# Add and GELU on 1024 x 4096: stores moved to ScalarE's queue, and every transfer in rows of 4 KB

## The chip, the cores and the metric

The kernel runs on one core of a Trainium2 chip. The metric is the device time of a run in microseconds. Each profile is of one execution; its span goes from the first to the last instruction, and the device time of that execution is a little longer than the span.

## The reference

```python
def reference(x, y):            # both float32, 1024 x 4096
    z = x + y
    return 0.5 * z * (1 + np.tanh(np.sqrt(2 / np.pi) * (z + 0.044715 * z ** 3)))
```

It is one elementwise chain: two tensors of 16.78 MB are read and one of 16.78 MB is written. The tanh form is computed as z * sigmoid(2 * sqrt(2/pi) * (z + 0.044715 z^3)), which is the same function.

## The kernel before

The 1024 rows are spread over 128 partitions, 8 rows to each, so that a partition owns 32768 elements that lie together in memory (128 KB). The elements of a partition are cut twice.

For the transfers they are cut into tiles by the list `sizes` (L43): 1024, 1024, 2048, then six tiles of 4096, then 2048, 1024, 512, 512 elements per partition, 13 tiles in all. A tile of 4096 elements is 2 MB, and one of its transfers has 128 rows of 16 KB. `load_x` (L71) loads a tile of x into a buffer of its own, which nothing else uses. `load_y` (L75) loads into one of four buffers of 4096 elements; a buffer is used again once its adds are done. `store` (L82) writes the x tile, which by then holds the result.

For the computation they are cut into chunks of at most 1024 elements. Each chunk passes five steps: `add` (L92), z = x + y, on Pool (GpSimd) for all but the first two and last two chunks, which VectorE adds; `sq` (L97), a scaled square on ScalarE into one of four PSUM buffers; `stt` (L100), (square + c1) * z on VectorE; `sig` (L105), the sigmoid on ScalarE; and `mul` (L108), sigmoid * z on VectorE, which puts the result into the x tile.

The order on every engine is written out by hand in four lists (L111 to L131) and kept as written. SyncE's list `sp` holds all transfers: x and y loads of tile after tile, and between them the stores. `LEAD` (8192 elements) says when: a store is put behind the loads that reach at least that far beyond it. VectorE's and ScalarE's lists come from one loop over i: VectorE gets `stt(i)`, `mul(i-1)` and, for the few chunks that Pool leaves, `add(i+3)`; ScalarE gets `sig(i)` and `sq(i+2)`. An instruction whose input is not there holds up everything behind it on its engine.

Of the kernel before, what the change touches and what calls it, by code (L numbers as in the profile page):

```python
# [1 line left out]

# [1 line left out]

# [4 lines left out]


@with_exitstack
def kernel(
    ctx: ExitStack,
    tc: tile.TileContext,
    x: bass.AP,
    y: bass.AP,
    out: bass.AP,
):

    nc = tc.nc
    P = nc.NUM_PARTITIONS
    fp32 = mybir.dt.float32
    act = mybir.ActivationFunctionType
    alu = mybir.AluOpType  # L30

    N, D = x.shape
    assert N % P == 0
    NB = N // P
    TOT = NB * D

    c1 = 2.0 * math.sqrt(2.0 / math.pi)
    root = math.sqrt(c1 * 0.044715)

    LEAD = 8192  # L40
    CH = 1024
    YB = 4
    sizes = [1024, 1024, 2048] + [D] * (NB - 2) + [2048, 1024, 512, 512]  # L43
    assert sum(sizes) == TOT
    starts = [sum(sizes[:t]) for t in range(len(sizes))]
    T = len(sizes)

    def hbm(ap, t):
        v = ap.rearrange("(p n) d -> p (n d)", p=P)
        return v[:, starts[t] : starts[t] + sizes[t]]  # L50

    chunks = []
    for t in range(T):
        o = 0
        while o < sizes[t]:
            f = min(CH, sizes[t] - o)
            chunks.append((t, o, f))
            o += f
    C = len(chunks)
    last = {t: c for c, (t, _, _) in enumerate(chunks)}  # L60
    by_pool = set(range(2, C - 2))

    xpool = ctx.enter_context(tc.tile_pool(name="xz", bufs=1))
    ypool = ctx.enter_context(tc.tile_pool(name="y", bufs=YB))
    ppool = ctx.enter_context(
        tc.tile_pool(name="w", bufs=4, space=bass.MemoryType.PSUM)
    )

    xt, yb, yt, wt = {}, {}, {}, {}

    def load_x(t):  # L71
        xt[t] = xpool.tile([P, sizes[t]], fp32, tag=f"x{t}", name=f"x{t}")
        nc.sync.dma_start(out=xt[t], in_=hbm(x, t))  # L73

    def load_y(t):  # L75
        n, o = divmod(starts[t], D)
        if o == 0:
            yb[n] = ypool.tile([P, D], fp32, tag="y", name=f"y{n}")
        yt[t] = yb[n][:, o : o + sizes[t]]
        nc.sync.dma_start(out=yt[t], in_=hbm(y, t))  # L80

    def store(t):  # L82
        nc.sync.dma_start(out=hbm(out, t), in_=xt[t])  # L83

    def z(c):
        t, o, f = chunks[c]
        return xt[t][:, o : o + f]

    def add(c):
        t, o, f = chunks[c]  # L90
        eng = nc.gpsimd if c in by_pool else nc.vector
        eng.tensor_add(out=z(c), in0=z(c), in1=yt[t][:, o : o + f])  # L92

    def sq(c):
        f = chunks[c][2]
        wt[c] = ppool.tile([P, CH], fp32, tag="w", name=f"w{c}")[:, :f]
        nc.scalar.activation(out=wt[c], in_=z(c), func=act.Square, scale=root)  # L97

    def stt(c):
        nc.vector.scalar_tensor_tensor(  # L100
            out=wt[c], in0=wt[c], scalar=c1, in1=z(c), op0=alu.add, op1=alu.mult
        )

    def sig(c):
        nc.scalar.activation(out=wt[c], in_=wt[c], func=act.Sigmoid)  # L105

    def mul(c):
        nc.vector.tensor_mul(out=z(c), in0=wt[c], in1=z(c))  # L108


    sp, pool, dve, acts = [], [], [], []  # L111
    s = 0
    for t in range(T):
        sp += [(load_x, t), (load_y, t)]
        while s < T and starts[s] + sizes[s] + LEAD <= starts[t] + sizes[t]:
            sp.append((store, s))
            s += 1
    sp += [(store, t) for t in range(s, T)]
    for c in range(C):
        if c in by_pool:  # L120
            pool.append((add, c))
    for i in range(-3, C + 1):
        if 0 <= i < C:
            dve.append((stt, i))
            acts.append((sig, i))
        if 0 <= i - 1 < C:
            dve.append((mul, i - 1))
        if 0 <= i + 3 < C and i + 3 not in by_pool:
            dve.append((add, i + 3))
        if 0 <= i + 2 < C:  # L130
            acts.append((sq, i + 2))  # L131

    needs = {
        load_x: lambda t: [],
        load_y: lambda t: [
            (add, c)
            for c, (i, _, _) in enumerate(chunks)
            if starts[t] % D == 0 and starts[i] // D == starts[t] // D - YB
        ],
        add: lambda c: [(load_y, chunks[c][0]), (load_x, chunks[c][0])],  # L140
        sq: lambda c: [(add, c)] + ([(mul, c - 4)] if c >= 4 else []),
        stt: lambda c: [(sq, c)],
        sig: lambda c: [(stt, c)],
        mul: lambda c: [(sig, c)],
        store: lambda t: [(mul, last[t])],
    }
    queues = [sp, pool, acts, dve]
    done = set()
    with tc.manual_schedule():
        one = xpool.tile([P, 1], fp32, tag="one", name="one")  # L150
        nc.vector.memset(one, 0.0)  # L151
        nc.scalar.activation(out=one, in_=one, func=act.Sigmoid)  # L152
        while any(queues):
            moved = False
            for q in queues:
                while q and all(n in done for n in needs[q[0][0]](q[0][1])):
                    fn, arg = q.pop(0)
                    fn(arg)
                    done.add((fn, arg))
                    moved = True  # L160
                    if q is not sp:
                        break
            assert moved, [q[:1] for q in queues]


# [1 line left out]
_INS = ['x', 'y']  # L167
_OUTS = [((1024, 4096), 'float32')]


# [23 lines left out]
```

## Time and profile before

| | |
|---|---|
| time, median of 2 runs | 126.73 us (126.62 to 126.85) |
| the profiled execution | 126.61 us |
| its span | 124.8 us |
| VectorE busy | 79.1 us, 71 instructions |
| Pool busy | 67.4 us, 33 instructions |
| ScalarE busy | 64.2 us, 68 instructions |
| DMA | 50.33 MB, 96.7% of 16 engines' span |
| one transfer of 2 MB, issue to landing (median) | x 18.5, y 23.3, store 14.0 us |

In the profile DVE is VectorE, ACT is ScalarE, POOL is GpSimd, and SP is SyncE; SPq is SyncE's queue of transfers. A number such as L92 is a line of the kernel. The rows of digits are 40 equal slices of the span, each digit the busy share in tenths, with the moved GB/s beneath. In a table by windows each row begins with the window in us and its length, then the busy time of VectorE, ScalarE and Pool with the instructions in it, then the TensorE clock, the DMA share and the GB/s. A row of a group shows how often it ran, its total busy time, the mean ns of one, and the idle time ahead of it with what ended it.

### The profile page before, as it was taken

To read this page: it belongs to the slowest core of one execution; us is meant where nothing else is said; L and a number is where in the kernel's file an instruction comes from. 1 tells how busy PE (TensorE), PEld (TensorE's weight loads), DVE (VectorE), ACT (ScalarE), POOL (GpSimd) and SP (SyncE) were. 2 spreads that over 40 slices of the span, in tenths; PEclk is the share of its full clock that TensorE was granted. 3 is DMA by queue.
4 is the path that set the end of the run, shared out by engine and by line. 5 is a ranking of instruction groups with operands and counts; after the bars stand their busy time and mean duration, and the time that the engine had idled before them with its cause. 6 is when DMAs were issued, how large, how long until landed. Compare 5 with 4: busy or idle time off the path is not lost.

```text
span 124.8 us, 301 instructions
## 1 busy us (share of the span) xinstructions
DVE 79.1 (63%) x71; ACT 64.2 (51%) x68; POOL 67.4 (54%) x33
## 2 busy tenths in 40 slices
DVE  0159259049979970299703996059930699899960
ACT  4036084068857820578206881088800887684610
POOL 0000670599799603996049950699207998960000
DMA  4999999999899999999999999999999999999494
GB/s 88 417 437 452 433 431 420 425 420 420 345 461 433 425 415 415 431 441 431 425 425 441 420 425 431 441 436 425 425 412 410 417 415 411 450 420 425 184 392 165
DMA packets 5618, 50.35 MB, mean 403 GB/s; under 512 B 624, under 2 KB 624, under 8 KB 2544
## 3 DMA queue, kind: packets, MB, share of 16 engines
q1 hardware_dynamic: 5616, 50.33, 96.7%
q14 instruction: 2, 0.02, 0.0%
HBM read 33.55 MB, written 16.78 MB: 403 GB/s over the span
## 4 chain that ended last, share of the span: by engine, by line
DMA 64%; POOL 15%; DVE 11%; SPq 3%; ACT 2%; issue 2%; POOLq 0%
DMA y<-in_y_dram 64%; POOL x L92 15%; DVE x L108 5%; DVE w L100 5%; SPq L73 2%; ACT w L97 2%; DVE x L92 1%; SPq L80 1%; ACT w L105 0%; SPq L83 0%; POOLq L92 0%
## 5 line engine op out<-in xcount | busy, mean ns | idle before, releaser
L92 POOL TENSOR_TENSOR x<-x,y 128x1024 f32<-128x1024 f32 x29 | 67.2, 2346 | 43.7 <-DMA y<-in_y_dram 43.7
L100 DVE SCALAR_TENSOR_TENSOR w<-w,x 128x1024 f32<-128x1024 f32 (+1 forms) x33 | 39.5, 1198 | 34.3 <-ACT w L97 34.3
L97 ACT ACTIVATE w<-x 128x1024 f32<-128x1024 f32 (+1 forms) x33 | 33.1, 1002 | 51.5 <-POOL x L92 45.1
L108 DVE TENSOR_TENSOR x<-w,x 128x1024 f32<-128x1024 f32 (+1 forms) x33 | 39.0, 1181 | 0.1
L105 ACT ACTIVATE w<-w 128x1024 f32<-128x1024 f32 (+1 forms) x33 | 31.6, 958 | 3.5 <-DVE w L100 3.4
L92 DVE TENSOR_TENSOR x<-x,y 128x1024 f32<-128x1024 f32 (+1 forms) x4 | 4.9, 1231 | 6.3 <-DMA y<-in_y_dram 6.3
L152 ACT ACT_TABLE_LOAD x1 | 1.3, 1283 | 0.7 <-PEq L178 0.7
L151 DVE MEMSET one<- 128x1 f32 x1 | 0.1, 59 | 0.8 <-PEq L178 0.8
L178 POOL MEMSET const-float32-0.0<- 128x1 f32 x1 | 0.1, 98 | 0.2 <-issue 0.2
L152 ACT ACTIVATE one<-one 128x1 f32<-128x1 f32 x1 | 0.2, 202 | 0.0
L178 POOL MEMSET const-bfloat16-1.0<- 128x1 bf16 x1 | 0.1, 101 | 0.0
L178 POOL MEMSET const-uint8-127<- 128x1 uint8 x1 | 0.1, 101 | 0.0
L178 POOL MEMSET const-float32-1.0<- 128x1 f32 x1 | 0.1, 98 | 0.0
## 6 DMA issues: line engine op xcount, KB each, us to landing
x<-in_x_dram SPq DMA_DIRECT2D x6, 2048.0 KB, 18.5
y<-in_y_dram SPq DMA_DIRECT2D x6, 2048.0 KB, 23.3
out_dram<-x SPq DMA_DIRECT2D x6, 2048.0 KB, 14.0
x<-in_x_dram SPq DMA_DIRECT2D x2, 1024.0 KB, 12.3
y<-in_y_dram SPq DMA_DIRECT2D x2, 1024.0 KB, 14.3
out_dram<-x SPq DMA_DIRECT2D x2, 1024.0 KB, 7.0
x<-in_x_dram SPq DMA_DIRECT2D x3, 512.0 KB, 5.4
y<-in_y_dram SPq DMA_DIRECT2D x3, 512.0 KB, 6.2
```

Of the source, the lines that this page charges most:

```text
L73: nc.sync.dma_start(out=xt[t], in_=hbm(x, t))
L80: nc.sync.dma_start(out=yt[t], in_=hbm(y, t))
L92: eng.tensor_add(out=z(c), in0=z(c), in1=yt[t][:, o : o + f])
L97: nc.scalar.activation(out=wt[c], in_=z(c), func=act.Square, scale=root)
L100: nc.vector.scalar_tensor_tensor(out=wt[c], in0=wt[c], scalar=c1, in1=z(c), op0=alu.add, op1=alu.mult)
L105: nc.scalar.activation(out=wt[c], in_=wt[c], func=act.Sigmoid)
L108: nc.vector.tensor_mul(out=z(c), in0=wt[c], in1=z(c))
L151: nc.vector.memset(one, 0.0)
L152: nc.scalar.activation(out=one, in_=one, func=act.Sigmoid)
L178: nc = _bacc.Bacc("TRN2", target_bir_lowering=False, num_devices=1)
```

## The change

`sizes` becomes 32 tiles of 1024 elements, so that each transfer is 512 KB in 128 rows of 4 KB, and a tile is a chunk. `store` is issued by ScalarE's queue in place of SyncE's. SyncE's list then holds loads alone, and `LEAD` is gone. ScalarE's list gets the stores: `store(i-3)` after `sq(i+2)`, and the last two at the end. The buffers of y still hold 4096 elements, four tiles each. The five steps of a chunk, their engines and their order stay as they are, with all chunks now 1024 elements long; before, the last two had 512.

```diff
-    LEAD = 8192
     CH = 1024
     YB = 4
-    sizes = [1024, 1024, 2048] + [D] * (NB - 2) + [2048, 1024, 512, 512]
+    sizes = [CH] * (TOT // CH)
...
     def store(t):
-        nc.sync.dma_start(out=hbm(out, t), in_=xt[t])
+        nc.scalar.dma_start(out=hbm(out, t), in_=xt[t])
...
     sp, pool, dve, acts = [], [], [], []
-    s = 0
     for t in range(T):
         sp += [(load_x, t), (load_y, t)]
-        while s < T and starts[s] + sizes[s] + LEAD <= starts[t] + sizes[t]:
-            sp.append((store, s))
-            s += 1
-    sp += [(store, t) for t in range(s, T)]
...
         if 0 <= i + 2 < C:
             acts.append((sq, i + 2))
+        if 0 <= i - 3 < C:
+            acts.append((store, i - 3))
+    acts += [(store, t) for t in range(C - 2, C)]
```

## The prediction

> **What bounds the kernel now.** I read the page's first parts, then busy time by windows, then the queue's waits and the groups. The page first: engine shares, and the DMA rows in 40 slices of 3.12 us.
>
> ```profile
> span 124.8 us, 301 instructions
> DVE 79.1 (63%) x71; ACT 64.2 (51%) x68; POOL 67.4 (54%) x33
> ...
> DMA  4999999999899999999999999999999999999494
> GB/s 88 417 437 452 433 431 420 425 420 420 345 461 433 425 415 415 431 441 431 425 425 441 420 425 431 441 436 425 425 412 410 417 415 411 450 420 425 184 392 165
> ...
> q1 hardware_dynamic: 5616, 50.33, 96.7%
> ```
>
> No compute engine passes 63%; the 16 DMA engines are full from the second slice to the thirty-seventh. Three tensors of 16.78 MB (50.33 MB) have to pass, so only the rate, the head and the tail can move the time. The windows, with the DMA share and GB/s in the last two columns, separate these:
>
> ```profile
> 4.00:6.50 2.50, 0.61 (x1) 0.00 (x0) 0.00 (x0) 1.00 1.03 421
> 30.00:36.00 6.00, 5.93 (x6) 4.15 (x5) 5.13 (x4) 1.00 1.00 385
> 36.00:38.00 2.00, 1.20 (x2) 1.68 (x2) 2.00 (x2) 1.00 1.13 475
> 48.00:60.00 12.00, 7.70 (x7) 7.67 (x8) 9.26 (x4) 1.00 1.01 433
> ...
> 100.00:103.00 3.00, 3.00 (x4) 2.63 (x4) 3.00 (x2) 1.00 0.99 406
> ...
> 116.00:118.00 2.00, 2.00 (x3) 1.79 (x3) 0.00 (x0) 1.00 0.28 119
> 118.00:122.00 4.00, 2.57 (x4) 0.76 (x2) 0.00 (x0) 1.00 0.98 396
> 122.00:124.80 2.80, 0.00 (x0) 0.00 (x0) 0.00 (x0) 1.00 0.37 139
> ```
>
> Clean stretches of 16 KB rows give 433 GB/s. The first loads, in 4 KB rows, give 421; 100 to 103 us, which mixes 4 and 8 KB rows, gives 406. Where the first stores follow loads the rate dips to 385 for 6 us and then catches up at 475. The last 8.8 us carry 119x2.0 + 396x4.0 + 139x2.8 = 2.21 MB. The 48.12 MB before that took 116.0 less a head of 2.5 us (the first slice's 88 GB/s x 3.12 us = 0.275 MB, at 421 worth 0.65 us, so data flows as if from 2.5): 113.5 us, a mean of 424.
>
> The transfer queue's waits:
>
> ```profile
> SPq L83 <- DVE x L108: 86.0, 12, 14.1
> SPq L73 <- DMA y<-in_y_dram: 5.4, 1, 5.4
> ```
>
> The queue spends most of its time standing at a store until `mul` has finished, which costs nothing while earlier transfers fill the engines. The second row matters more: a load of x into a buffer of its own needs no data, yet waited for a y load to land. [...] The groups give the durations used below:
>
> ```profile
> L92 POOL TENSOR_TENSOR x<-x,y 128x1024 f32<-128x1024 f32 x29 | 67.2, 2346 | 43.7 <-DMA y<-in_y_dram 43.7
> L100 DVE SCALAR_TENSOR_TENSOR w<-w,x 128x1024 f32<-128x1024 f32 x31 | 38.1, 1231 | 34.3 <-ACT w L97 34.3
> L108 DVE TENSOR_TENSOR x<-w,x 128x1024 f32<-128x1024 f32 x31 | 37.6, 1213 | 0.0
> L97 ACT ACTIVATE w<-x 128x1024 f32<-128x1024 f32 x31 | 31.9, 1028 | 51.5 <-POOL x L92 45.1 <-DVE x L92 6.4
> L105 ACT ACTIVATE w<-w 128x1024 f32<-128x1024 f32 x31 | 30.5, 983 | 2.1 <-DVE w L100 2.0
> ```
>
> [...] The trace has nothing of two queues (all data is in q1). [...]
>
> **The change, part by part.** *Rows of 4 KB.* All 96 transfers become 512 KB. In the trace one 4 KB row takes 159 ns on its engine, a 16 KB row 611, so four small ones cost 25 ns (4%) more. By the rows' durations alone the small ones give 16 x 4096 B / 159 ns = 412 GB/s; what was moved gives 406 to 421. I take 415, and keep 406 and 424 as bounds.
>
> *Semaphores and prefetch.* In the order of the changed program, loads run up to tile 7, then every third transfer is a store. [...]the x load of tile s+10 waits for the landing of store s, and the y load of tile t for the x load of tile t-2. Four or five loads of 512 KB can then be queued, over two tiles' time, so the engines stay fed as long as the store returns in time. A tile takes 3 x 0.524 MB / 415 = 3.79 us. Store s stands in ScalarE's queue behind `sq` of tile s+5, so it is issued 2.35 (Pool add) + 1.03 (`sq`) + about 0.4 = 3.8 us after tile s+5 lands. From then to the landing of tile s+9, the last load that is free to go, are 4 x 3.79 = 15.2 us. The store should take 2.7 fixed (a lone 512 KB store in the tail of before takes 4.0 to land, 1.26 of it data) and two data times, since it shares, 5.2 us; the freed load needs another 2.7. 3.8 + 5.2 + 2.7 = 11.7 < 15.2: covered by 3.5 us.
>
> *Issuing on ScalarE.* 32 issues at 0.33 to 0.69 us (the range on SyncE; ScalarE's isn't shown), I take 0.4. Queued behind each is `sig`, on which `mul` waits. Per tile 1.03 + 0.98 + 0.4 = 2.4 us of 3.8: hidden in the body at either bound; VectorE (2.44) and Pool (2.35) are under 3.8 too. Against before, SyncE no longer stands at a store, but as the queue was full that frees no time.
>
> *The tail.* This is where I see the loss. Let E be the landing of y31, the last load. ScalarE's order is fixed: sq30, store 25, sig29, sq31, store 26, sig30, store 27, sig31, stores 28 to 31. VectorE, not Pool, adds tiles 30 and 31, and has add31 ahead of stt29. So after E: add31 ends at 1.2, stt29 at 2.5, sig29 at 3.5, sq31 at 4.5, and only then does store 26 go, whose `mul` ended long ago. VectorE goes on: mul28 3.7, stt30 4.9, mul29 6.1, stt31 7.3; sig31 ends at 8.3; then stores 28 to 31 are issued. Store 25 goes near E+1, 26 near 4.5, 27 near 6: the engines are mostly idle until then. From 8.3: 2.7 fixed + 4 x 1.26 data + 0.8 to the end of the span (as before's last landing at 124.0 to 124.8) = E+16.85.
>
> *The sum.* By the last byte of the loads, 64 loads and 25 stores have passed: 89 x 0.524 = 46.66 MB. At 415 that is 112.4 us. With the head 2.5 and 1.0 from last byte to landing (an estimate, within the 2.7), E = 115.9; the span is 132.7. The profiled run of before took 126.61 for a span of 124.8, so 1.8 is added: 134.5 us. That run lies 0.1 below the median of 126.73, which I neglect. Against before: the body sheds 1.46 MB (-3.4 us), the rows cost 2.4 (415 for 424), and the tail is 17.85 instead of 8.8 (+9.05). At 424 the result is 132.1, at 406 it is 137.2.
>
> **The rivals.** *Alternating directions costs.* If switching from load to store packet by packet keeps the dip's 385 GB/s: 46.66/385 = 121.2, in all 143.7. For it: the dip. Against: 475 just after, so what a switch one way loses, the way back returns.
>
> *Loads starve behind the semaphores.* If a store takes 12 us to land because loads are ahead of it on every engine, five tiles need 3.8 + 12 + 2.7 + 1.3 = 19.8, so 3.95 us per tile, 0.16 more for some 26 tiles: 138.7. It decides from 8.7 us of landing time.
>
> *Directions overlap (the other side).* If loads and stores use separate paths and the body reaches the 475 of that one window: 98.2 us, and 17.3 of tail: 119.8, faster. It decides from 456 GB/s (124.2). [...]475 was a catch-up.
>
> *Nearly no change.* If 4 KB rows run at the 433 of long ones and the tail is 1.6 us shorter (landing at 0.3, and stores 25 to 27 spread better): 107.8 + 2.5 + 16.2 + 1.8 = 128.3.
>
> **How the numbers follow.** Likeliest case 0.54 (132 to 137), costly alternation 0.17, starved loads 0.12, no change 0.10, overlap 0.07. Two per cent is about what a measurement of this kernel can tell from no change, 124.2 to 129.3. So faster 0.07, same 0.10, slower 0.83. The range 129.0 to 143.5 leaves out the overlap, most of the no-change case and what of the alternation lies above it.
>
> **What would show it.** Right: two data queues, with a DMA share near 1.0 and 406 to 424 GB/s until about 114 us, then some 17 us in which the slices alternate low and full, and ScalarE waiting for VectorE's stt with stores behind. Compute groups keep their durations. Wrong: slices above 440 in the body (overlap), 4 KB packets far longer than 159 ns (alternation), or SyncE waiting for store landings with a share below 0.95 (starved). A tail that is full to the end would make my largest term wrong.

## The result and the profile after

The changed kernel takes 131.75 us (131.67 to 131.82, 2 runs) against 126.73: a ratio of 1.0395, 95% interval 1.0349 to 1.0442. It is slower by 4%. The forecast was 134.5 with a range of 129.0 to 143.5; the time lies in it, just under the 132 to 137 of the likeliest case. The profiled execution took 131.82 us for a span of 130.0.

The first parts of its page, in the same form as before:

```profile
span 130.0 us, 345 instructions
DVE 79.9 (61%) x69; ACT 64.0 (49%) x66; POOL 65.9 (51%) x32
...
DMA  4999999999999999999999999999999999954594
GB/s 102 417 418 408 410 413 407 403 421 418 422 417 418 422 421 418 421 416 423 418 418 421 416 423 420 416 420 417 420 423 417 420 416 422 420 218 161 214 404 188
...
q1 hardware_dynamic: 9216, 33.56, 64.0%
q10 hardware_dynamic: 4608, 16.78, 31.7%
```

The data now passes through two queues, loads in q1 and stores in q10. The busy times of the compute engines are what they were, ScalarE's included, though it now issues 32 transfers. The body is level between 403 and 423 GB/s, where before it moved between 345 and 461. The new thing stands at the end: slices 36, 37 and 38 at 218, 161 and 214 GB/s. The windows say how much that is (last two columns: DMA share and GB/s):

```profile
110.00:115.00 5.00, 3.29 (x3) 0.89 (x1) 0.00 (x0) 1.00 0.88 360
115.00:124.00 9.00, 8.84 (x9) 5.01 (x6) 0.00 (x0) 1.00 0.53 211
124.00:128.00 4.00, 0.55 (x1) 0.00 (x0) 0.00 (x0) 1.00 1.02 408
```

From 115 to 124 us VectorE is busy for 8.84 of 9 us and the DMA engines for half of the time. Measured against 419 GB/s, the first two rows lack 0.7 + 4.5 = 5.2 us of transfer time. The hole of the kernel before, 119 GB/s from 116 to 118 us, lacks 1.4 against its mean of 424. In these windows the tail lost 3.7 us more than it did. Counted from 110 us to the end of each span, where the means are 271 and 314 GB/s, it is 3.2. The timeline shows what those microseconds held (start, duration, engine, line, operation; ACTq is ScalarE's sequencer, which issues its transfers):

```profile
111.71 1.23 DVE L91 TENSOR_TENSOR x<-x,y 128x1024 f32<-128x1024 f32 x1 [6.28 <-DMA y<-in_y_dram]
...
115.36 1.23 DVE L91 TENSOR_TENSOR x<-x,y 128x1024 f32<-128x1024 f32 x1 [0.16 <-DMA y<-in_y_dram]
...
117.76 1.01 ACT L104 ACTIVATE w<-w 128x1024 f32<-128x1024 f32 x1 [1.71 <-DVE w L99]
117.77 0.34 ACTq L82 DMA_DIRECT2D out_dram<-x  x1
...
122.29 1.01 ACT L104 ACTIVATE w<-w 128x1024 f32<-128x1024 f32 x1 [1.25 <-DVE w L99]
122.29 2.91 ACTq L82 DMA_DIRECT2D out_dram<-x  x4
```

The first two rows are the adds of tiles 30 and 31; the second is released by the last load. The next two are the sigmoid of tile 29 and, with it, the store of tile 26. The last two are the sigmoid of tile 31 and the last four stores, 28 to 31: the first of them is issued at 122.29 us, the last at 124.6, when its product is done. Until 122.29 us the engines get one store at a time.

### The profile page after: what moved, and what is told of

Same layout as the page of the kernel before. It is cut to its first block, busy times and chain, and to the rows that moved or that the text cites. A ratio compares the mean times of both kernels' runs of the same rounds, so it can differ in the third digit from the quotient of the medians.

```text
span 130.0 us, 345 instructions
## 1 busy us (share of the span) xinstructions
DVE 79.9 (61%) x69; ACT 64.0 (49%) x66; POOL 65.9 (51%) x32
## 4 chain that ended last, share of the span: by engine, by line
DMA 81%; DVE 7%; POOL 4%; SPq 3%; issue 1%; POOLq 0%; DVEq 0%; ACT 0%
DMA y<-in_y_dram 41%; DMA x<-in_x_dram 30%; DMA out_dram<-x 10%; POOL x L91 4%; DVE x L107 3%; DVE w L99 3%; SPq L72 1%; SPq L79 1%; DVE x L91 1%; POOLq L91 0%; DVEq L91 0%; ACT w L96 0%
## 5 line engine op out<-in xcount | busy, mean ns | idle before, releaser
L91 POOL TENSOR_TENSOR x<-x,y 128x1024 f32<-128x1024 f32 x28 | 65.7, 2347 | 42.8 <-DMA y<-in_y_dram 42.6
L99 DVE SCALAR_TENSOR_TENSOR w<-w,x 128x1024 f32<-128x1024 f32 x32 | 39.4, 1232 | 30.7 <-ACT w L96 30.6
L96 ACT ACTIVATE w<-x 128x1024 f32<-128x1024 f32 x32 | 32.9, 1027 | 50.8 <-POOL x L91 44.1
L107 DVE TENSOR_TENSOR x<-w,x 128x1024 f32<-128x1024 f32 x32 | 38.9, 1216 | 0.0
L104 ACT ACTIVATE w<-w 128x1024 f32<-128x1024 f32 x32 | 31.5, 985 | 7.7 <-DVE w L99 7.4
L91 DVE TENSOR_TENSOR x<-x,y 128x1024 f32<-128x1024 f32 x4 | 4.9, 1225 | 13.1 <-DMA y<-in_y_dram 13.1
```

The lines of the kernel that those rows point to most:

```text
L99: nc.vector.scalar_tensor_tensor(out=wt[c], in0=wt[c], scalar=c1, in1=z(c), op0=alu.add, op1=alu.mult)
```

## The experiments

Two things were to be settled. Which part of the loss belongs to the rows, the second queue and the tail? And in the tail: are finished stores held up in ScalarE's queue, as the prediction argued, or is too little left to store when the last load lands? Ratios are to the kernel before, run beside each.

**Short rows alone.** The kernel before, with each of its transfers cut:

```diff
-        nc.sync.dma_start(out=xt[t], in_=hbm(x, t))
+        nc.sync.dma_start(out=xt[t], in_=hbm(x, t), max_dma_last_dim=4096)
```

and the same on the y loads and the stores.

> The kernel before with its 13 tiles, one queue and its order, but every transfer cut into rows of 4 KB (a 2 MB transfer has 512 rows in place of 128). It has the row length alone. Theory (rows cost a little everywhere): the clean stretches fall from 433 to about 418 GB/s as in the changed kernel, so 48 MB take 2 to 4 us longer: 128.7 to 130.7 us, a 4 KB row still 159 ns. Rival (the whole loss is in the tail and the flat 419 GB/s of the changed kernel comes from mixing loads with stores): the body keeps 433 GB/s and the time stays at 126.7.

128.05 us, ratio 1.0114 (1.0059 to 1.0168). The windows:

```profile
12.00:30.00 18.00, 8.50 (x9) 7.16 (x9) 10.52 (x5) 1.00 1.03 409
50.00:56.00 6.00, 2.41 (x3) 3.11 (x4) 5.84 (x3) 1.00 1.03 424
118.00:120.00 2.00, 2.00 (x4) 1.31 (x3) 0.00 (x0) 1.00 0.86 352
```

Short rows cost 1.1%, some 1.4 us, under the 2 to 4 that the theory gave, so its range is missed by a little; the rival's unchanged time and 433 GB/s are further off. The first window holds loads alone, the second stores: both below the 433 of long rows, the loads further. The third row bears on the small sum: the hole of the tail, 119 GB/s with long rows, is 352 here. That the slower body fills part of it is my reading, not tested by itself.

**The second queue alone.** The tiles and long rows of before, the stores on ScalarE three chunks behind `sq`; SyncE's list loses its stores, as in the changed kernel:

```diff
-        nc.sync.dma_start(out=hbm(out, t), in_=xt[t])
+        nc.scalar.dma_start(out=hbm(out, t), in_=xt[t])
...
+        acts += [(store, t) for t in range(T) if last[t] == i - 3]
+    acts += [(store, t) for t in range(T) if last[t] > C - 3]
```

> The tiles and long rows of the kernel before, with the stores issued by ScalarE three chunks behind sq, as in the changed kernel. It has the second queue and the mixing alone. Theory (mixing loads and stores is free, the tail costs): 425 to 433 GB/s until the last load lands at about 113 us, then a tail of 12 to 14 us with half-empty slices, 127 to 129 us. Rival (alternation costs): the body falls below 410 GB/s and the time goes to 131 us or more. Rival (mixing gains): the body is above 440 GB/s.

126.91 us, ratio 1.0053 (1.0032 to 1.0075), just under the 127 to 129 expected. From 48 to 60 us it moves 437 GB/s, and 427 over the 100 us from 4 to 104:

```profile
48.00:60.00 12.00, 9.28 (x8) 7.77 (x8) 7.07 (x4) 1.00 1.02 437
4.00:104.00 100.00, 65.62 (x57) 54.08 (x56) 63.06 (x28) 1.00 1.01 427
```

The kernel before has 433 and 425 in the same two windows. Loads and stores under way together thus neither cost nor gain anything to speak of; both rivals on this fall. The 0.5% by which the run is longer goes with a hole near its end, taken up below.

**Stores held back.** The changed kernel, its stores five tiles later, the backlog released together before the sigmoid of tile 29:

```diff
+        if i == C - 3:
+            acts += [(store, t) for t in range(C - 11, C - 4)]
...
-        if 0 <= i - 3 < C:
-            acts.append((store, i - 3))
-    acts += [(store, t) for t in range(C - 2, C)]
+        if 0 <= i - 8 < C - 11:
+            acts.append((store, i - 8))
+        if i >= C - 2:
+            acts.append((store, i - 2))
+    acts += [(store, t) for t in range(C - 1, C)]
```

> The changed kernel with its stores held back five tiles more (store of tile i-8 in place of i-3), and the seven held ones, 21 to 27, released together ahead of the sigmoid of tile 29; 28 to 31 follow as their products are done. Nothing else. Theory (in the changed kernel the loads end too late, with too few stores left to cover the last tiles' arithmetic): the last load lands about 109 us, the engines stay full over the tail, 50.33 MB at 417 GB/s, 126 to 127 us. Rival (4 KB rows and mixing are the whole loss): the time stays at 130 us or above.

128.02 us, ratio 1.0121 (1.0054 to 1.0188). That is 3.7 us less than the changed kernel by the medians, 3.5 by the ratios, and 1 above the expectation.

```profile
span 126.1 us, 346 instructions
...
DMA  3999999999999999999999999999999999899994
GB/s 83 418 422 407 413 411 407 409 412 409 407 414 417 418 422 421 416 420 418 422 418 420 420 420 418 416 421 417 421 417 418 422 420 417 339 403 404 408 403 182
...
105.61 1.22 DVE L91 TENSOR_TENSOR x<-x,y 128x1024 f32<-128x1024 f32 x1 [5.59 <-DMA y<-in_y_dram]
```

The half-empty slices are gone; what is left is one at 339. The add of tile 30, which waits for its y load in every variant, starts at 105.61 us in place of 111.71. Five stores of 0.524 MB at 419 GB/s are 6.3 us: holding five stores back let the loads end 6 us sooner, and the held stores covered the arithmetic. The time is now that of short rows alone (1.0114).

**Stores moved up.** The changed kernel, with the opposite edit:

```diff
+        if 0 <= i - 2 < C:
+            acts.append((store, i - 2))
         if 0 <= i < C:
             acts.append((sig, i))
...
-        if 0 <= i - 3 < C:
-            acts.append((store, i - 3))
-    acts += [(store, t) for t in range(C - 2, C)]
+    acts += [(store, t) for t in range(C - 1, C)]
```

> The changed kernel with each store moved up ScalarE's list, ahead of the sigmoid two tiles later (store i-2 before sig i), so that no store stands behind a sigmoid that waits for VectorE. Nothing else. Theory as the prediction had it (finished stores held up behind sig29, sq31, sig30 make the idle slices): 2 us or more are saved, below 129.8 us. Rival (the tail is set by the last load and by VectorE's seven steps after it; earlier stores only delay the last load by their own bytes): between 131 and 133 us.

132.59 us, ratio 1.0476 (1.0419 to 1.0532). It is not faster, as it would be if held-up stores were the cause. That it is slower than the changed kernel is only indicated, since the intervals overlap by a little. The timeline and the windows:

```profile
114.25 1.23 DVE L91 TENSOR_TENSOR x<-x,y 128x1024 f32<-128x1024 f32 x1 [6.23 <-DMA y<-in_y_dram]
```

```profile
118.00:120.00 2.00, 2.00 (x3) 0.59 (x1) 0.00 (x0) 1.00 0.65 262
120.00:122.00 2.00, 2.00 (x3) 1.91 (x2) 0.00 (x0) 1.00 0.00 0
122.00:124.00 2.00, 2.00 (x3) 1.04 (x2) 0.00 (x0) 1.00 0.65 262
```

No finished store stands behind a waiting sigmoid now, and the engines still run empty, for two whole microseconds from 120 to 122, because VectorE has not finished the next product. And the add of tile 30 starts 2.5 us later than in the changed kernel, which is what two stores take at 419 GB/s: stores sent earlier took the loads' time.

The landings say how much was left to store when the last load landed. In the changed kernel it is seven stores, 3.7 MB, at 115.3 us; with stores held back twelve, 6.3 MB, at 109.1; here five, 2.6 MB, at 117.7. The kernel before has 6.3 MB left at 109.3 us. Among the three with short rows, the less is left, the longer the run.

**Less arithmetic at the end.** The changed kernel without `sq`, `stt`, `sig` and `mul` of the last four tiles, so that x + y is stored for them:

```diff
-        if 0 <= i < C:
+        if 0 <= i < C - 4:
             dve.append((stt, i))
             acts.append((sig, i))
-        if 0 <= i - 1 < C:
+        if 0 <= i - 1 < C - 4:
...
-        if 0 <= i + 2 < C:
+        if 0 <= i + 2 < C - 4:
...
-        store: lambda t: [(mul, last[t])],
+        store: lambda t: [(mul if t < C - 4 else add, last[t])],
```

> The changed kernel without the arithmetic of its last four tiles: tiles 28 to 31 are added and stored, their sq, stt, sig and mul are left out (their output is z). Transfers, queues and rows stay. Theory (the tail of the changed kernel is VectorE's and ScalarE's arithmetic after the last load, with too few stores left to cover it): the half-empty slices go, the engines stay full to the end, 126 to 128 us. Rival (the loss is the rows and the mixing): 131 us or more.

126.99 us, ratio 1.0104 (1.0068 to 1.0139).

```profile
116.07 1.23 DVE L91 TENSOR_TENSOR x<-x,y 128x1024 f32<-128x1024 f32 x1 [2.21 <-DMA y<-in_y_dram]
```

```profile
DMA  4999999999999999999999999999999999999992
GB/s 85 420 421 409 409 410 409 409 420 418 420 418 420 421 422 420 418 418 420 418 420 417 418 421 420 421 417 421 421 418 418 418 420 420 418 420 414 420 420 102
```

The add of tile 31 starts at 116.07 us, later than the 115.36 of the changed kernel, and the run is still shorter: with nothing but an add to compute after the last load the engines are full to the end. Again the ratio is near that of the rows. So of the 4.0% the rows are about 1.1 and the tail about 2.8, shown by two different edits that remove it (2.7 and 2.9).

**A search for a better kernel.** Three runs tried to close the holes of the two kernels with long rows. With `LEAD` raised from 8192 in the kernel before, stores stand later in SyncE's queue:

```diff
-    LEAD = 8192
+    LEAD = 12288
```

> The kernel before with LEAD 12288 in place of 8192, so that each store stands one 2 MB tile later in SyncE's queue and the loads end sooner. Nothing else. Theory (what counts is how many bytes are left to store when the last load lands): the hole at 116 to 118 us, 119 GB/s, worth 1.45 us, closes: ratio to before about 0.988, 125.2 us. Rival (later stores only shift the hole): ratio 0.997 to 1.003.

> The kernel before with LEAD 16384: two 2 MB tiles later. Theory: the engines cannot be fuller than full, so as with 12288, ratio 0.985 to 0.992. Rival ([...]the loads run ahead of the adds and stall on the four y buffers): ratio above 1.0.

126.02 us, ratio 0.9998 (0.9964 to 1.0032) with 12288, and 125.54, ratio 0.9966 (0.9938 to 0.9994) with 16384. Both expectations, 0.988 and 0.985 to 0.992, are missed. In the trace of the first the hole is gone:

```profile
116.00:118.00 2.00, 0.00 (x0) 0.00 (x0) 0.00 (x0) 1.00 0.97 410
118.00:120.00 2.00, 0.00 (x0) 0.00 (x0) 0.00 (x0) 1.00 0.98 400
120.00:122.00 2.00, 0.00 (x0) 0.00 (x0) 0.00 (x0) 1.00 0.59 229
```

yet the time is that of before. The last row points to a part of the reason. The 16 engines did not finish together: the last store's parts land over 1.9 us here, and over 0.6 in the kernel before, where some engines still worked through the hole while the others waited (the parts of the 2 MB store under way there landed from 116.2 to 119.0 us). Closing the hole moved part of the waiting to the end. The rest stays open. The two traced executions do differ by 1.1 us (126.61 and 125.48), but the runs of the kernel before that the ratio uses spread from 124.85 to 126.70 us, with a median of 126.06, and no trace tells whether all of them have the hole. The gain of the second, 0.3%, is the only one found.

The third took the run with the second queue alone, whose own trace has a hole of 49 and 131 GB/s from 110 to 114 us, and moved its stores up:

```diff
+        acts += [(store, t) for t in range(T) if last[t] == i - 2]
         if 0 <= i < C:
             dve.append((stt, i))
...
-        acts += [(store, t) for t in range(T) if last[t] == i - 3]
-    acts += [(store, t) for t in range(T) if last[t] > C - 3]
+    acts += [(store, t) for t in range(T) if last[t] > C - 2]
```

> Long rows and two queues (the run of the second queue alone), with each store moved ahead of the sigmoid two chunks after its tile's last. In that run the loads had ended by 107 us and the engines stood almost empty from 110 to 114 us (49 and 131 GB/s) while the 2 MB store of the tile before the last four waited behind sigmoids. Theory (here a finished store is held with nothing else left to move, so freeing it does help): the hole closes, 2 to 3 us less than that run, ratio to before 0.98 to 0.99. Rival (as with the early stores in 4 KB rows, the last load only comes later): ratio 1.005 or more.

125.93 us, ratio 1.0002 (0.9971 to 1.0033): about 0.5% better than without the edit, not the 2 to 3 us expected.

```profile
110.00:112.00 2.00, 1.09 (x2) 0.98 (x1) 0.00 (x0) 1.00 0.97 398
112.00:114.00 2.00, 2.00 (x3) 1.22 (x2) 0.00 (x0) 1.00 1.05 442
114.00:116.00 2.00, 2.00 (x3) 0.65 (x2) 0.00 (x0) 1.00 0.83 352
116.00:118.00 2.00, 2.00 (x3) 1.74 (x3) 0.00 (x0) 1.00 0.25 106
```

The hole closed where it was and opened again at 116 us, where VectorE is busy throughout: the last tiles' arithmetic with nothing left to store, once more. With that edit a second queue is no worse than one, to within 0.3%.

**Which short rows cost.** The kernel before with rows of 4 KB on its loads alone (the edit of the first experiment without the stores):

> The kernel before with rows of 4 KB for the loads alone; its stores keep their long rows. Theory (in the run with 4 KB rows throughout, stretches of loads alone ran at about 409 GB/s with rows of 163 ns, stretches of stores at 423 with 159, so loads bear most of the cost): ratio 1.008 to 1.012 of the 1.0114 that all rows cost. Rival (every row costs alike): two thirds of it, 1.007 or less.

127.53 us, ratio 1.0129 (1.0054 to 1.0204). By its middle value the loads alone bear as much as all rows together did, but the interval is too wide to exclude the rival's 1.007, so this is not shown.

**Short rows without arithmetic.** The kernel of the first experiment, with the lists of `add`, `sq`, `stt`, `sig` and `mul` taken out, a store that waits for its x load, and y loads that wait for no buffer:

> The kernel with 4 KB rows throughout and one queue, with all arithmetic left out: x and y are loaded, x is stored as it came. It asks why loads of 4 KB rows run at 419 GB/s in the first 10 us and at about 409 later. Theory (VectorE, ScalarE and Pool working on the same on-chip memory slow the writing of the loads): without arithmetic loads stay at 419 or above and a row at 159 ns. Rival (it lies in the transfers themselves): 405 to 412 and 163 ns as with arithmetic.

One run, 128.16 us.

```profile
4.00:10.00 6.00, 0.00 (x0) 0.00 (x0) 0.00 (x0) 1.00 1.03 419
12.00:32.00 20.00, 0.00 (x0) 0.00 (x0) 0.00 (x0) 1.00 1.03 410
50.00:56.00 6.00, 0.00 (x0) 0.00 (x0) 0.00 (x0) 1.00 1.02 421
```

With no engine computing, loads alone still fall from 419 to 410 GB/s after the first 10 us, and stores run at 421. The theory falls: without arithmetic these loads were no faster (410 GB/s, against 409 with it in the run with short rows alone). What slows them is not settled. The time of this one run is also that of the same transfers with arithmetic (128.05), so there the arithmetic seems fully hidden.

## Why the prediction was right, step by step

*What bounds it.* Right: transfers, with the compute engines at their old durations (Pool's add 2347 ns for 2346).

*The rows.* Right in sign and near in size. I took 415 GB/s for the body against 424; from 4 to 112 us it was 417 against 425, which is 2.1 us where I put 2.4. The kernel with short rows alone grew by 1.4 only.

*Semaphores and prefetch.* Right in its result. SyncE did wait for stores to land, with this row among its waits,

```profile
SPq L72 <- DMA out_dram<-x: 16.2, 6, 5.0
```

and the x loads of tiles 10 to 14 each went some 0.02 us after the landing of the store ten tiles before (store 4 landed at 41.63 us, the x load of tile 14 was issued at 41.64); from tile 15 on the pairs were others than forecast. In the traces of the two kernels at most eight transfers were under way at once. But the share stayed at 1.03 meanwhile (40 to 110 us), since a store landed 6.6 us after its issue (median), more than the 5.2 I put, but below the 8.7 from which the starved case would decide.

*The tail.* Right in place and sign, too large by 2.1 us: from the last load's landing (115.3, with 115.9 forecast) to the end are 14.8 us, not 16.85. With the 0.6 by which the landing came sooner this is the whole error of 2.7. The terms that were mis-sized are these. VectorE's steps follow each other every 1.13 us, not 1.2, so stt31 ended 7.0 us after the landing, not 7.3. I had the stores wait for the end of sig31; the first of the last four was issued at its start, 122.29 us, 1.0 earlier than I had it for that reason. From there to the landing of the last were 6.5 us, not 7.7, because the 2.7 of fixed time was misread: the store that I called a lone one had a store of 1 MB ahead of it. In the changed kernel's tail a store that is alone lands 2.6 us after its issue, 1.4 more than its data takes. From the last landing to the end were 1.2 us, not 0.8.

One omission cost nothing by luck. Store 31 also has to wait for mul31, which ends 1.2 us after sig31 and which my chain leaves out; but stores 28 to 30 kept the engines full meanwhile (408 GB/s from 124 to 128 us).

The step that named the cause was wrong in part. I had "only then does store 26 go, whose `mul` ended long ago", behind sq31 and 4.5 us after the landing. The store was indeed held: its product was done by 105.4 us. But it went 2.5 us after the landing, with the start of sig29 and ahead of sq31 (118.68), so it stood behind the wait for stt29 and not behind sq31. And freeing the stores gained nothing: each store sent sooner made the loads land later by about its own 1.25 us, as the two edits of the order show (five held back, tile 30 begins 6.1 us sooner; two moved up, 2.5 us later), and after the last load VectorE's chain decides: six steps to the end of stt31, then the last two products. What governs in these kernels is how much is left to store when the last load lands. By the ratios, holding stores back gained some 3.5 us and taking the arithmetic out 3.7.

*The rivals.* Alternation costs: no, 419 GB/s from 60 to 100 us in 4 KB rows, where from 60 to 62 us the two queues moved 105 rows of loads and 100 of stores, and 437 in long ones. Directions overlap: no, over 100 us the long rows in two queues gave 427 against 425; windows of 2 us above 456 (467 and 500) stand beside low ones (49 and 336). Before the result no run had shown this; the 0.07 that I gave it was an estimate. Starved loads: no. Nearly no change: it needed both long-row speed and a tail of some 16 us. The tail was even shorter, 14.8, but the body ran at 417, not 433.

## What to carry to other kernels

In this kernel, which transfers bound, the order of loads and stores cost nothing that shows in the middle (427 GB/s from 4 to 104 us against 425, with long rows) and decided the end (holding stores back gave 3.7 us): keep enough stores in hand to cover the arithmetic that follows the last load, and let loads go first. How much that gives has to be measured: in the kernel with long rows and one queue, which already had 6.3 MB in hand, still later stores gave nothing or 0.3%. A finished store that waited was no loss in the changed kernel (with its stores moved up the time was 132.59 us against 131.75), so look in the windows for a low DMA share, not for waiting stores. To tell the row length from the order, cut the rows alone and leave everything else.

## What the runs showed of the hardware

Two things were not expected. ScalarE's sequencer issued transfers while its activations ran: in the changed kernel a store and the sigmoid ahead of it start together at 122.29 us, and ScalarE's busy time stays at 64.0 us with 32 more issues, so they cost it nothing here. And loads of 4 KB rows ran slower by themselves (413 to 420 GB/s by run from 4 to 10 us, 408 to 410 after that) than mixed with stores, which gave 419 over 40 us of the run with held-back stores:

```profile
12.00:34.00 22.00, 19.20 (x18) 15.56 (x17) 20.33 (x9) 1.00 1.03 410
60.00:100.00 40.00, 24.84 (x22) 20.23 (x21) 25.80 (x11) 1.00 1.03 419
```

The first row is loads alone, the second loads and stores together, in one execution. In the changed kernel a 4 KB row took 164 ns (median) from 12 to 22 us, where loads run alone at 408 GB/s, and 159 from 30 to 110 us, at 419. The reason was not found.
